# A recurrent block and its output product, put into one written order

## Chip, cores and metric

The kernel runs on one core of a Trainium2 chip. The metric is the device time of one execution in microseconds (us). The engines are TensorE (PE in the profile; PEld is its weight load), VectorE (DVE), ScalarE (ACT), GpSimd (POOL) and SyncE (SP), which here issues all DMAs.

## The reference, cut to what matters

A trunk of two layers on 1024 tokens of 1024 features, float32. Layer 0 is a gated linear recurrence, layer 1 a banded attention; a squared-ReLU MLP of 4096 hidden features follows each. The change lies in layer 0's recurrent block and in the first steps of both MLPs:

```python
def recurrent_block(x, w_in, conv_w, conv_b, w_gate, b_gate, lam, w_out):
    u = x @ w_in                                    # x is rmsnorm(h, a_norm)
    gate, rec = u[..., :D_RNN], u[..., D_RNN:]
    rec = causal_depthwise_conv(rec, conv_w, conv_b)   # four taps over tokens
    h = rg_lru(rec, w_gate, b_gate, lam)
    return (jax.nn.gelu(gate) * h) @ w_out

def rg_lru(x, w_gate, b_gate, lam):                 # eight blocks of 128 features
    g = einsum('bsnd,nde->bsne', x, w_gate) + b_gate
    r, i = sigmoid(g[..., :LRU_BW]), sigmoid(g[..., LRU_BW:])
    log_a = -LRU_C * r * softplus(-lam)
    a = exp(log_a)
    b = sqrt(-expm1(2.0 * log_a)) * (i * x)
    return associative_scan over tokens of h = a * h + b

h = h + recurrent_block(rmsnorm(h, a_norm[l]), ...)
h = h + square(relu(rmsnorm(h, mlp_norm[l]) @ w_up)) @ w_down
```

## The kernel before

Features lie on partitions (128 at a time, `NF` = 8 tiles of them), tokens along the free dimension, in two halves of 512 (`H2`). Every float32 product is made of three float32r matmuls: each operand is split into a high half (a ScalarE copy to float32r) and a low half (a VectorE or GpSimd subtraction); `mm` (lines 319 to 324) multiplies high by high, low by high, high by low into one PSUM bank. A 128x128 weight block against 512 tokens is thus three matmuls, and a whole output tile from 1024 features and 1024 tokens 48.

Order. Most of the kernel is ordered by the framework's scheduler, which simulates the engines with its own costs and takes instructions by the order in which the program traced them. Two stretches are written as chains for a planner of the kernel's own (`Plan`, line 65): each chain is a generator that issues instructions and yields the time from which it goes on; `Flag` and `Sema` are its events and counts; the instructions go into the engines' queues in the planned order. Before, these are the start (lines 526 to 543) and the attention.

The recurrent block before:

- Start: each token tile is loaded, split into halves with the norm's gain but without the norm, and multiplied at once with the first two `w_in` blocks (`first_blocks`). Beside it GpSimd squares the tokens, VectorE adds them up (line 490), an all-ones matmul sums over partitions (line 494), and ScalarE and VectorE make R, minus the reciprocal root (lines 497 to 506).
- `rec_proj` (line 547) makes one block of `rec`: 48 matmuls, then per half VectorE takes the product out of PSUM times -R (line 557) into a tile with three columns of history (lines 554, 556).
- `conv` (line 569): one ScalarE activation and three VectorE steps per half (line 578), then the split.
- `gates` (line 585) and `lru` (line 603): gate products, sigmoid, tanh, exponential, square root on ScalarE, the rest on VectorE, two multiplies on GpSimd (lines 598, 616), and the scan (line 618). All per half.
- `gelu_gate` (line 624): 48 matmuls, per half times -R (line 630), gelu, times the recurrence's result (line 632), split.
- Weights: `prepared` (line 264) splits them; for most `w_in` blocks the low half is GpSimd's (line 288).
- `Out.whole` (line 716): `w_out` product; `first` adds the residual, `last` squares and sums for the next norm, and `combine` (line 690) makes the operands of the MLP from a pair of tiles.

The MLP uses a seven-product (Strassen-like) scheme: `mlp_up` (line 737) needs seven combinations XT[0..6] of its input, each for four pairs of tiles, and per quarter four weight tiles A11 to A22 and sums of them made by GpSimd (lines 766 to 769). It asks for both norms R first (line 740), and so for their two all-ones matmuls (lines 353, 354).

## Time and profile before

| | us |
|---|---|
| median of 3 runs (2179.67 to 2182.55) | 2181.44 |
| profiled execution | 2182.72 |
| its span, first to last instruction | 2180.9 |

| engine | busy us | share of the span |
|---|---|---|
| TensorE matmul | 2112.1 | 97% |
| TensorE weight load | 1742.7 | 80% |
| VectorE | 1579.6 | 72% |
| ScalarE | 1114.8 | 51% |
| GpSimd | 661.4 | 30% |

Matmuls are pipelined, so a row of the timeline is longer than the step to the next one, and busy TensorE is not TensorE at its peak: the step between starts is what counts. The rows the text rests on stand below, in groups.

### The profile page before, as it was taken

What the parts mean: (1) busy time and instruction counts of PE and PEld (TensorE: products, weight loads), DVE (VectorE), ACT (ScalarE), POOL (GpSimd) and SP (SyncE); (2) the same over time, 40 slices, a digit from 0 to 9 for tenths busy, and PEclk for the clock granted to TensorE, in tenths of its full rate; (3) what the DMA queues carried; (4) which work ended last, traced back from release to release, by engine and by line L of the source; (5) the groups of instructions that cost most, each with busy time, mean ns of one, the idle gap of its engine ahead of it and who ended that gap; (6) DMA issues with size and microseconds to landing.
All of it is one profiled execution on the core that took longest, in us unless ns stands there. A gap on an engine that the chain in (4) does not pass through costs nothing.

```text
span 2180.9 us, 29620 instructions
## 1 busy us (share of the span) xinstructions
PE 2112.1 (97%) x9753; PEld 1742.7 (80%) x9753; DVE 1579.6 (72%) x2716; ACT 1114.8 (51%) x2030; POOL 661.4 (30%) x567
## 2 busy tenths in 40 slices
PE   7898998999999999998999999999899999999999
PEld 5776786888888888886888888878688888888887
DVE  7788866877777786555777777777687777777843
ACT  4576745444444445454666666665444344444632
POOL 5354301333320000115666666651233333000000
PEclk8999999999999999999999999999999999999999
DMA  5111144444459785442333333353354444977832
GB/s 180 32 53 37 34 141 130 156 155 155 154 179 325 244 264 179 127 150 69 96 94 82 89 84 83 89 167 109 119 178 152 150 155 155 331 263 234 258 105 97
DMA packets 176746, 319.21 MB, mean 146 GB/s; under 512 B 20816, under 2 KB 23120, under 8 KB 176592
## 3 DMA queue, kind: packets, MB, share of 16 engines
q1 hardware_dynamic: 176592, 317.33, 45.3%
q8 instruction: 76, 1.25, 0.2%
q14 instruction: 78, 0.64, 0.1%
HBM read 219.73 MB, written 78.64 MB: 137 GB/s over the span
## 4 chain that ended last, share of the span: by engine, by line
PE 78%; DVE 10%; DMA 4%; ACT 3%; issue 3%; POOL 2%; SPq 0%; DVEq 0%; ACTq 0%; POOLq 0%
PE pj L322 12%; PE pj L324 11%; PE pj L323 11%; PE tp L323 6%; PE tp L322 6%; PE tp L324 6%; PE sc L322 5%; PE sc L323 5%; PE sc L324 4%; PE tp L1178 2%; DVE c L578 2%; PE po L1206 1%; DMA s<-in_xT 1%; PE po L1205 1%; PE sc L1153 1%
## 5 line engine op out<-in xcount | busy, mean ns | idle before, releaser
L322 PE MATMUL pj<-h,wh 128*128 128x512 f32 x1269 | 510.3, 402 | 4.4 <-ACT h L338 1.6
L323 PE MATMUL pj<-l,wh 128*128 128x512 f32 x1269 | 497.1, 392 | 1.6 <-DVE l L339 1.6
L324 PE MATMUL pj<-h,wl 128*128 128x512 f32 x1269 | 496.8, 392 | 0.0
L733 ACT ACTIVATE wh<-raw 128x512 fp32r<-128x512 f32 x352 | 221.5, 630 | 335.8 <-PE tp L323 77.7
L734 DVE TENSOR_TENSOR wl<-raw,wh 128x512 fp32r<-128x512 f32 x352 | 276.5, 786 | 106.2 <-ACT wh L733 101.7
L322 PEld LDWEIGHTS pj<-h,wh 128*128 128x128 f32 x1269 | 240.0, 189 | 51.0 <-DVE s L782 2.4
L324 PEld LDWEIGHTS pj<-h,wl 128*128 128x128 f32 x1269 | 239.4, 189 | 51.5
L323 PEld LDWEIGHTS pj<-l,wh 128*128 128x128 f32 x1269 | 240.4, 189 | 43.7 <-DVE l L339 2.5
L323 PE MATMUL tp<-l,wh 128*128 128x512 f32 x657 | 257.7, 392 | 2.2 <-DVE l L336 2.1
L322 PE MATMUL tp<-h,wh 128*128 128x512 f32 x657 | 258.2, 393 | 0.4 <-ACT wh L733 0.4
L324 PE MATMUL tp<-h,wl 128*128 128x512 f32 x657 | 257.6, 392 | 0.0
L322 PE MATMUL sc<-h,wh 128*128 128x512 f32 x569 | 224.1, 394 | 6.8 <-DVE rec L557 6.8
L323 PE MATMUL sc<-l,wh 128*128 128x512 f32 x569 | 223.9, 393 | 3.0 <-DVE l L336 3.0
L324 PE MATMUL sc<-h,wl 128*128 128x512 f32 x569 | 223.4, 393 | 0.0
L336 DVE TENSOR_TENSOR l<-raw,h 128x512 fp32r<-128x512 f32 x224 | 153.6, 693 | 30.0 <-ACT h L335 28.8
L766 POOL TENSOR_TENSOR raw<-raw,raw 128x512 f32<-128x512 f32 x32 | 52.2, 1632 | 397.7 <-DVE wl L734 376.8
L748 ACT ACTIVATE s<-s 128x512 f32<-128x512 f32 x128 | 80.2, 629 | 170.9 <-DVE s L747 170.9
L335 ACT ACTIVATE h<-raw 128x512 fp32r<-128x512 f32 x224 | 137.2, 620 | 56.8 <-DMA raw<-hid 33.1
L323 PEld LDWEIGHTS tp<-l,wh 128*128 128x128 f32 x657 | 124.6, 190 | 29.7 <-DVE l L336 3.3
L322 PEld LDWEIGHTS tp<-h,wh 128*128 128x128 f32 x657 | 124.4, 189 | 27.3 <-ACT wh L733 1.0
L324 PEld LDWEIGHTS tp<-h,wl 128*128 128x128 f32 x657 | 124.4, 189 | 26.6 <-DVE wl L734 0.6
L288 POOL TENSOR_TENSOR wl<-raw,wh 128x512 fp32r<-128x512 f32 x74 | 106.1, 1439 | 118.0 <-ACT wh L285 111.6
(262 smaller groups left out, 3971.5 us busy)
## 6 DMA issues: line engine op xcount, KB each, us to landing
hid<-s SPq DMA_DIRECT2D x224, 256.0 KB, 2.0
raw<-hid SPq DMA_DIRECT2D x224, 256.0 KB, 3.6
raw<-in_w_down SPq DMA_DIRECT2D x192, 256.0 KB, 3.5
raw<-in_w_up SPq DMA_DIRECT2D x128, 256.0 KB, 2.6
s<-in_w_down SPq DMA_DIRECT2D x64, 256.0 KB, 4.5
raw<-in_w_kv SPq DMA_DIRECT2D x32, 256.0 KB, 3.3
raw<-in_w_in SPq DMA_DIRECT2D x31, 256.0 KB, 3.1
od<-ev SPq DMA_DIRECT2D x48, 128.0 KB, 2.3
```

What stands on the lines that cost most here:

```text
L288: eng.tensor_tensor(wl, raw, wh.bitcast(F32), ALU.subtract)
L322: pe.matmul(ps, lhsT=wh, rhs=xh, start=start, stop=False, skip_group_check=more)
L323: pe.matmul(ps, lhsT=wh, rhs=xl, start=False, stop=False, skip_group_check=more)
L324: pe.matmul(ps, lhsT=wl, rhs=xh, start=False, stop=stop, skip_group_check=more)
L335: act.activation(h, src, AF.Copy)
L336: dve.tensor_tensor(l, src, h.bitcast(F32), ALU.subtract)
L578: dve.scalar_tensor_tensor(ct, rec[h][:, k : k + H2], vec[:, V_CW + k, n : n + 1], ct, ALU.mult, ALU.add)
L733: act.activation(wh, raw, AF.Copy)
L734: dve.tensor_tensor(wl, raw, wh.bitcast(F32), ALU.subtract)
L748: act.activation(out, out, AF.Square)
L766: pool.tensor_tensor(raw[A11], raw[A11], raw[A21], ALU.add)
L1178: pe.transpose(pt[:, g * P : (g + 1) * P], sc[:, (kb - kb0) * P : (kb - kb0 + 1) * P], ident)
```

## The change

- The start, all eight blocks, the `w_out` product and the pair work for the MLP become one planned stretch. It ends before the last pair's combinations.
- Tokens are normalised before they are split (`halve`), so products come out of PSUM finished: no `rec` tile, no times -R. Squares move to ScalarE. The first three `w_in` blocks (two `rec`, one gate) are multiplied together, half by half. Warm-up matmuls go from 9 to 24.
- PSUM is four tiles of 1024 columns; `conv`, `lru`, `gate` and the output's add work on 1024 columns at a time, the convolution straight from PSUM. They share `NB` = 7 buffers (`bf`) and `NX` = 4 (`xf`) of 1024 columns. `+ 1` goes to ScalarE. Low halves of `w_in` weights go from GpSimd to VectorE.
- 84 of the `w_out` matmuls (two tiles, seven of eight features) come before the last Y, and the last two tiles are multiplied side by side.
- Two weight tiles of the first MLP quarter are fetched and split in the stretch; the other sums are traced before the last pair's combinations. Pools opened later reuse the first ones' memory, with waits by tile.
- For both MLPs: one ScalarE copy less in a pair's combinations, the weight sums in another order, and R asked for after four products.

```diff
-SQA = ((6, 1), (7, 1))
-WARM = 9
+NB = 7
+NX = 4
+NRAW_A = 3
+NW_A = 10
+WARM = 24
...
+    def square(k, h):
+        yield arrived[k, h]
+        if (k, h) == (0, 1):
+            yield normal[0,]
+        elif h:
+            yield squared[k - 1, h]
...
+    def halve(k, h):
+        yield normal[h,]
...
+        dve.tensor_tensor(x, x, R[h], ALU.mult)
+        yield plan.use("dve", d_(H2))
...
+        act.activation(hi, x, AF.Copy, scale=g)
...
+        dve.scalar_tensor_tensor(lo, x, g, hi.bitcast(F32), ALU.mult, ALU.subtract)
...
+    def conv(n, ps):
+        yield plan.now + LAT
+        if n >= 2:
+            yield posted[n - 2,]
+        yield bs
+        c = bf("c")
+        act.activation(
+            c, ps, AF.Identity,
+            scale=vec[:, V_CW + 3, n : n + 1], bias=vec[:, V_CB, n : n + 1],
+        )
+        yield plan.use("act", a_(T))
+        for k in range(3):
+            d = 3 - k
+            dve.scalar_tensor_tensor(
+                c[:, d:], ps[:, : T - d], vec[:, V_CW + k, n : n + 1], c[:, d:], ALU.mult, ALU.add
+            )
+            yield plan.use("dve", d_(T)) - LAT
+        pss.release(plan.t + LAT)
+        yield plan.t + LAT
+        yield bs
+        yield bs
+        ch, cl = bf("ch", F32R), bf("cl", F32R)
...
+    def lru(n, psr, psi):
+        yield plan.now + LAT
+        for _ in range(3):
+            yield bs
+        posted[n,].set(plan.t)
+        r, i, t = bf("sig"), bf("sig"), bf("tanh")
+        c = C[n][0]
+        act.activation(r, psr, AF.Sigmoid, bias=vec[:, V_BR, n : n + 1])
...
+        act.activation(i, psi, AF.Sigmoid, bias=vec[:, V_BI, n : n + 1])
...
+        act.activation(t, r, AF.Tanh, scale=sp4[:, n : n + 1])
...
+        pool.tensor_tensor(i, i, c, ALU.mult)
+        bs.release(plan.use("pool", p_(T)))
...
+        act.activation(r, r, AF.Exp, scale=sp8[:, n : n + 1])
+        act.activation(r, r, AF.Identity, bias=ones[:, 0:1])
...
+        dve.scalar_tensor_tensor(u, t, 1.0, r, ALU.add, ALU.mult)
+        dve.scalar_tensor_tensor(u, u, 4.0, r, ALU.subtract, ALU.mult)
...
+        act.activation(t, t, AF.Sqrt, scale=0.25)
...
+        dve.tensor_scalar(r, u, -0.5, -1.0, ALU.mult, ALU.add)
...
+        dve.scalar_tensor_tensor(t, t, -1.0, u, ALU.mult, ALU.mult)
...
+        pool.tensor_tensor(t, t, i, ALU.mult)
...
+        dve.tensor_tensor_scan(u, r, t, 0.0, ALU.mult, ALU.add)
...
+    def gate(n, ps):
...
+        act.activation(g, ps, AF.Gelu_apprx_tanh)
...
+        yield hidden[n,]
+        dve.tensor_tensor(g, g, HID[n], ALU.mult)
...
+    def tensor():
...
+        for n in range(1, NF + 1):
+            if 2 <= n + 1 < NF:
+                yield pss
+                ps = bank2()
+                yield from block(ps, widx[NF + n + 1], X, allk, True, True)
+                plan.start(conv(n + 1, ps))
+            m = n - 1
+            yield conved[m,]
+            yield pss
+            yield pss
...
+            plan.start(lru(m, *pair))
+            if m:
+                yield pss
+                ps = bank2()
+                yield from block(ps, widx[m], X, allk, True, True)
+                plan.start(gate(m, ps))
...
+        for j in range(2):
+            yield pss
+            ahead[j] = bank2()
+            yield from block(ahead[j], widx["out", j], Y, range(NF - 1), True, False)
...
+    def ahead_weights():
+        yield out_y[NF - 2,]
+        for x in (A11, A12):
...
+            dma(raw, w_up[0, 0, x])
...
-            b12, b21, b22 = sf(), sf(), sf()
+            b12, b22, t1, t3 = self.scratch()
+            self.XT[0][i] = split(x11, ga)
+            self.XT[1][i] = split(x21, gb)
...
-            self.XT[0][i] = split(x11, ga)
-            self.XT[1][i] = split(b21)
...
+            dve.scalar_tensor_tensor(t1, x21, gb, t1, ALU.mult, ALU.add)
+            self.XT[3][i] = split(t1, -1.0)
...
+    def up_sums(raw):
+        pool.tensor_tensor(raw[A11], raw[A11], raw[A21], ALU.add)
+        pool.tensor_tensor(raw[A21], raw[A21], raw[A22], ALU.add)
+        s1 = wsplit(raw[A21])
...
-        R = [o.r(0), o.r(1)]
+        R = []
...
+            if not R:
+                R.extend((o.r(0), o.r(1)))
...
+    first_stage.close()
+    rp = ctx.enter_context(tc.tile_pool(name="rp", bufs=NRAW, reuse_waits="tile"))
...
+    ws0 = up_weights(0, 0, FIRST_W)
+    sums0 = up_sums(ws0[0])
+    o1.combine(NF // 2 - 1)
```

In `FirstOut`, `result` adds a tile of the output to the residual, writes it to memory, squares and sums it; `combined` makes a pair's operands as `combine` does, as a chain of the plan.

## Rows read from the trace of the kernel before

**Rows 1.** The page: the span, and TensorE's busy tenths in 40 slices of the span.

```profile
span 2180.9 us, 29620 instructions
...
PE   7898998999999999998999999999899999999999
```

**Rows 2.** Busy time by stage, TensorE: stretch, length, busy (matmuls), clock, DMA share, GB/s.

```profile
0.00:57.95 57.95, 45.79 (x157) 0.88 0.52 176
57.95:281.33 223.38, 199.93 (x818) 0.95 0.14 46
281.33:350.39 69.06, 67.48 (x298) 1.00 0.42 127
350.39:390.00 39.61, 34.80 (x128) 0.87 0.40 136
372.40:1000.00 627.60, 626.86 (x2763) 1.00 0.56 185
1559.00:1584.00 25.00, 18.88 (x55) 0.80 0.36 119
```

**Rows 3.** The same view, blocks: PE, PEld, DVE, ACT, POOL busy, then the clock.

```profile
75.00:262.00 187.00, 170.58 (x707) 135.65 (x705) 159.61 (x213) 134.96 (x191) 85.62 (x53) 0.96 0.13 40
```

**Rows 4.** TensorE's waits, 0 to 400 us: us in total, times, longest.

```profile
PE po L494 <- DVE acc L490: 7.8, 1, 7.8
PE sc L322 <- DVE rec L557: 6.8, 3, 3.1
```

**Rows 5.** Groups by line, VectorE, 75 to 262: busy us, mean ns, idle before.

```profile
L578 DVE SCALAR_TENSOR_TENSOR c<-rec,vec,c 128x512 f32<-128x512 f32 x42 | 39.7, 944 | 0.9 <-ACT c L573 0.3
...
L632 DVE TENSOR_TENSOR s<-s,q 128x512 f32<-128x512 f32 x14 | 12.5, 913 | 0.0
...
L557 DVE SCALAR_TENSOR_TENSOR rec<-sc,rneg 128x512 f32<-128x512 f32 x5 | 3.4, 675 | 0.7 <-PE sc L324 0.7
```

**Rows 6.** Groups by line, ScalarE and GpSimd, 75 to 262.

```profile
L285 ACT ACTIVATE wh<-raw 128x512 fp32r<-128x512 f32 x23 | 13.9, 620 | 8.6 <-PE sc L323 5.5 <-PE tp L323 3.0
...
L592 ACT ACT_TABLE_LOAD x7 | 9.0, 1283 | 0.1
...
L616 POOL TENSOR_TENSOR tanh<-tanh,sig 128x512 f32<-128x512 f32 x15 | 26.4, 1776 | 65.7 <-DVE tanh L615 65.7
L566 POOL TENSOR_TENSOR gw<-graw,gw 128x256 fp32r<-128x256 f32 x5 | 6.6, 1327 | 6.1 <-ACT gw L563 6.1
```

**Rows 7.** Timeline, single instructions: start us, us, engine, line, operation.

```profile
5.66 1.04 POOL L481 TENSOR_TENSOR s<-x 128x512 f32<-128x512 f32 x1 [1.07 <-DMA x<-in_xT]
6.24 0.40 ACT L452 ACTIVATE w<-raw 128x256 fp32r<-128x256 f32 x1
7.17 0.41 DVE L454 TENSOR_TENSOR w<-raw,w 128x256 fp32r<-128x256 f32 x1
...
25.01 1.53 DVE L490 TENSOR_TENSOR acc<-acc,s 128x512 f32<-128x512 f32 x1
28.57 0.68 DVE L490 TENSOR_TENSOR acc<-acc,s 128x512 f32<-128x512 f32 x1
...
47.54 1.02 PE L494 MATMUL po<-acc,onesr 128*128 128x512 f32 x2
51.37 0.69 DVE L506 SCALAR_TENSOR_TENSOR rneg<-s,rneg 128x512 f32<-128x512 f32 x1
52.10 0.16 DVE L404 TENSOR_SCALAR e<-vec 128x8 f32<-128x8 f32 x1
...
266.76 1.26 DVE L618 TENSOR_TENSOR_SCAN q<-sig,q,tanh 128x512 f32<-128x512 f32 x1
```

**Rows 8.** Busy time by stage, all engines, the first 10 us.

```profile
0.00:10.00 10.00, 6.87 (x15) 4.27 (x15) 3.08 (x5) 4.30 (x7) 3.50 (x14) 1.00 0.67 208
```

**Rows 9.** Timeline, TensorE at the start of layer 1's MLP.

```profile
1565.12 0.50 PE L353 MATMUL po<-ah,onesr 128*128 128x512 f32 x1 [1.28 <-ACT ah L347]
...
1577.24 0.77 PE L353 MATMUL sc<-ah,onesr 128*128 128x512 f32 x1 [2.72 <-ACT ah L347]
```

More of the change, by code (lines that the diff above doesn't have):

```diff
@@ L1 @@
 import heapq
+import itertools
 from contextlib import ExitStack
@@ new lines, in tile_yoco_rglru_chunk_attention, with load_half, split_half @@
+    wsrc = [w_in[x] for x in worder] + [w_out[j] for j in range(NF)]
+    widx = {x: i for i, x in enumerate(worder)}
+    widx.update({("out", j): 2 * NF + j for j in range(NF)})
+    IN_G = (2, 3)
+    def load_half(i, y):
+        raw = blocks4(rawf())
+        dma(raw, wsrc[i][:, 4 * y : 4 * y + 4, :])
+        plan.start(split_half(i, y, raw), plan.load(4 * P))
+    def split_half(i, y, raw):
+        if i not in IN_G:
+            yield wss
+            yield wss
+        get = gr if i in IN_G else wr
+        wh, wl = blocks4(get("wh")), blocks4(get("wl"))
+        W[i, y] = wh, wl
+        act.activation(wh, raw, AF.Copy)
+        yield plan.use("act", a_(H2))
+        dve.tensor_tensor(wl, raw, wh.bitcast(F32), ALU.subtract)
+        last = plan.use("dve", d_(H2))
+        raws.release(last)
+        weighed[i, y].set(last)
@@ new lines, in block @@
+    def block(ps, i, Z, ks, start, stop):
+        for y in range(2):
+            mine = [k for k in ks if k // 4 == y]
+            if not mine:
+                continue
+            yield weighed[i, y]
+            for h in range(2):
+                for k in mine:
+                    if Z is Y:
+                        yield out_y[k,]
+                    w = W[i, y]
+                    mm(
+                        ps[:, hs(h)], (w[0][:, k % 4, :], w[1][:, k % 4, :]), Z[k][h],
+                        start and k == ks[0], stop and k == ks[-1],
+                    )
+                    yield plan.pe(3 * H2) - LAT
+            if i not in IN_G and mine[-1] % 4 == 3:
+                wss.release(plan.now)
+                wss.release(plan.now)
@@ L526, in tile_yoco_rglru_chunk_attention @@
-    with tc.manual_schedule(engines=set(ENG)):
-        idle = bank("sc")
-        wide = onesr.unsqueeze(1).broadcast_to([P, 4, P])
-        for x in range(WARM):
-            pe.matmul(idle, lhsT=onesr, rhs=wide, start=x == 0, stop=x == WARM - 1)
-        plan.start(loads())
-        for h in range(2):
-            for k in range(NF):
-                plan.start(halve(k, h))
-                plan.start(square(k, h))
-        for h in range(2):
-            plan.start(rstd(h))
-        plan.start(first_blocks())
-        plan.run()
@@ L639, in tile_yoco_rglru_chunk_attention @@
[L639 to L652 removed]
+                for x in range(3):
+                    yield weighed[x, k // 4]
+                    yield halved[k, h]
+                    w = W[x, k // 4]
+                    mm(recs[x][:, hs(h)], (w[0][:, k % 4, :], w[1][:, k % 4, :]), X[k][h], k == 0, k == NF - 1)
+                    yield plan.pe(3 * H2) - LAT
@@ new lines, in tensor @@
+        for _ in range(NG - 4 * NF - 4):
+            goods.release(plan.now)
+        plan.start(ahead_weights())
+        ahead = {}
+        for j in range(2):
+            yield pss
+            ahead[j] = bank2()
+            yield from block(ahead[j], widx["out", j], Y, range(NF - 1), True, False)
+        for j in range(NF - 2):
+            if j in ahead:
+                ps = ahead[j]
+                yield from block(ps, widx["out", j], Y, range(NF - 1, NF), False, True)
+            else:
+                yield pss
+                ps = bank2()
+                yield from block(ps, widx["out", j], Y, allk, True, True)
+            plan.start(o1.result(j, ps))
@@ L654, in out_order @@
+    FIRST_W = []
+    A11, A12, A21, A22 = range(4)
     def out_order(j0):
@@ L656, in out_order @@
         return full + [(j, h) for h in range(2) for j in range(NF - 2, NF)]
-    A11, A12, A21, A22 = range(4)
     class Out:
@@ L752, in mlp_up @@
             if q < NQ:
-                raw = [wload(w_up[layer, q, x]) for x in range(4)]
-                a11, a12, a22 = wsplit(raw[A11]), wsplit(raw[A12]), wsplit(raw[A22])
+                raw, (a11, a12), a22 = up_weights(layer, q) if ws is None else ws
+                ws = None
                 z, v = bank("pj"), bank("sc")
```

631 lines of the change are left out of this document (383 added, 248 removed).

## The prediction

> **What bounds the kernel now.** First the page's head and its slices: TensorE is busy 97% of the span and its row falls below 9 mostly in the first seven slices of 54.5 us, so what can be won lies where it is not dense [rows 1]. Then busy time by stage, the view that carries this prediction [rows 2]. Its second last row is the first MLP and what follows, with nothing in the way: 2763 matmuls in 627.6 us, 0.2271 us each at 512 columns. At that step the 1248 matmuls of the recurrent block and output product (768 for `w_in`, 96 for the gates, 384 for `w_out`) are 283.4 us. They end at 350 us. What each stretch takes beyond its matmuls:
>
> - 0 to 57.95 (144 matmuls beside nine of warm-up and four of the norm): 57.95 - 32.7 = 25.2 us
> - 57.95 to 281.33, the eight feature blocks (816): 223.4 - 185.3 = 38.1 us
> - 281.33 to 350.39, the output product (298): 1.4 us
> - 350.39 to 390, the hand-over to the MLP (128): 10.5 us
> - 1559 to 1584, the same hand-over in layer 1 (55): 12.5 us
>
> The third view says why the blocks are not dense: from 75 to 262 VectorE is busy 159.6 of 187 us, 85%, and TensorE's clock is down to 0.96 [rows 3]. The list of waits agrees: TensorE's longest there is for `rec` (line 557), VectorE's copy of a product out of PSUM, which every projection needs before its bank is free [rows 4].
>
> **The blocks, part by part.** A block is 108 matmuls, 24.5 us. I count what each engine has to do in it. A 1024-column instruction is not in the trace; I take the 512-column one plus the step from 256 to 512: ScalarE 0.40 to 0.62, so 1.06 us; VectorE 0.41 to 0.68, so 1.22 us; the scan 1.26, so 2.4 us; GpSimd 1.04 alone, so 2.1, or twice its mean of 1.78 beside VectorE, 3.55 us [rows 6, 7].
>
> VectorE: removed are the two `rec` products with the norm, the copy, the two products of the gelu input with the norm, and the `+ 1` (to ScalarE). Left are three convolution steps, the low half of c, two steps of u, one of t and the gate product, 8 x 1.22 = 9.8; the `r` step 0.7; the scan 2.4; and 512-column low halves, four of weights (up to now mostly GpSimd's) and two of Y, 6 x 0.68 = 4.1. Sum 17.0 us. To that comes what GpSimd costs it. The convolution step with two SBUF operands averages 0.944 us where PSUM-fed line 557 takes 0.675, and line 632 0.913 [rows 5]: some 35% on such instructions with GpSimd busy 85.6 of 187 us. GpSimd falls to two multiplies and one gate weight, 5.5 to 8.4 us of 24.5, and only 10.9 us of VectorE's list has two SBUF operands, since the convolution now reads PSUM. So +2.3: 19.3 of 24.5 us, 79%.
>
> ScalarE: nine 1024-column instructions 9.5, six halves 3.7, the gate weight 0.4, four table loads at 1.28 [rows 6] 5.1: 18.7 us, 76%. The table loads stay as many as before. No engine but TensorE fills the block.
>
> **The loop that is added.** One block's `lru` takes three of the seven 1024-column buffers; four are held by c of this block and c, ch, cl of the next. So the next `lru` starts after this one's scan, whatever TensorE does. Its length: table load and three activations 4.5; table load, exponential and `+ 1` 3.4 (the square root runs beside the next); two steps of u 2.4; r and t 1.9; GpSimd's multiply 2.1 to 3.55; scan 2.4: 16.7 to 18.2 us. Behind each of five changes of engine it can find another chain's instruction in the queue, one of about 1 us: 22 to 23. That is under 24.5, so the loop keeps up. The first turn has no gate product and is 13.6 us long, so it starts about 8.5 us late and wins 2 us a turn back; a PSUM bank is missed only from 8.6 us on (a gate product of 10.9 less 2.3 to the first sigmoid's end). At the end the last Y must come while TensorE does the last gate product and the 84 `w_out` matmuls put ahead of it: 10.9 + 19.1 = 30.0, against the loop 22, the gate product and its halves 3.2 and what is left of the lag, 0 to 5. I take 9 us lost in the blocks in place of 38.1: 4 at that end, 3 for lag, 2 for the first turn. Ends: nothing lost, and 53 us if the loop takes 31 (7 turns x 6.5 + 8 at the end).
>
> A rule of the Trainium skill speaks against the wide multiplies. What the trace shows: the same add of line 490 takes 1.53 us while GpSimd multiplies and 0.68 when it does not [rows 7]. The page "SBUF — State Buffer", section "Who interferes with whom", says that a VectorE instruction with two SBUF inputs and a GpSimd instruction that reads SBUF hold one shared port pair in turn, each for its whole length. By that, twice as long a multiply is twice as long a block for whoever comes second, and u, t and the scan could each wait 3.5 us; the time would be that of the slower rival below. The same section says that one SBUF input does not contend, and line 557 agrees.
>
> **The start.** Before, the first product starts on raw tokens as they come; now it waits for the norm. 208 GB/s came in over the first 10 us [rows 8], 2.1 MB, which is the eight half rows of the tokens. Square 0.62, add 0.68, then from the sum's matmul to the norm 4.5 us (47.54 to 52.06) [rows 7]: 16 us; product 0.68 and high half 0.7: first matmul at about 17.5. 24 warm-up matmuls cover until 9. Half the 144 matmuls, 16.4, and 2 for the lower clock after an idle stretch: 36. On SyncE's queue the second half rows stand behind the fourth weight load, which waits for one of three raw buffers, that is for the first split at about 12; at 1.26 us each they land by 22. The second half's norm comes when VectorE has done eight token products and low halves 10.9, seven adds 4.8, five weight halves 3.4, the norm 1.4 and half of some thirty constants at 0.16 [rows 7] 2.5, 23.0 after 16.5: with its first half 40.9. Then 16.4: 57.3. So this costs what it did; I take 57, 24 lost. Ends: 50 with no second wait, 66 if weights take half the early bandwidth (10 us) and each add meets a queue.
>
> **The output and the hand-over.** The product itself has 1.4 us to lose; its results are added at 1.22 us each 10.9 us apart, and a pair's combinations are eleven VectorE instructions of 0.69, 7.6 us in 21.8, so 1.4 stays; ends 0 and 6. At its end the two last results (2.4), a split (1.4) and the queues come to about 6 us; ready then are A11 and A12 and three of four pieces of two products, 18 matmuls, 4.1. 2 lost, 1 for the next pieces, 1.5 for the sums of the other two weights (their loads stand behind two result writes), 1.5 for the clock (0.87 in this stretch before [rows 2]): 6 in place of 10.5; ends 3 and 15. The DMAs moved are the same loads. They cost nothing while those 18 matmuls last.
>
> **Layer 1.** Norm sums are now asked for behind the first four products. TensorE waited 1.28 and 2.72 for their high parts [rows 9]; 4 us go, next late is the low half of the last tokens. 9 in place of 12.5; ends 5 and 14. One scalar copy less in a pair costs or wins nothing there.
>
> **Sum.** 25.2 to 24, 38.1 to 9, 10.5 to 6, 12.5 to 9: 38.3 us less. The profiled execution took 2182.72 (span 2180.9), 1.3 above the median of 2181.44. 2182.7 - 38.3 - 1.3 = 2143. The attention and MLP stretches have the same code and the same 0.2271.
>
> **Rivals.**
> 1. The added loop rules, slower. From 30 us on, 7 x 5.5 + 8 = 47 lost eats all (29.1 + 9.2 + 9). If u, r and t, and the scan each wait 3.5 us for GpSimd, 18.2 + 10.5 + 5 is 33.7; at 33 the blocks lose 67.5 where I have 9: 2143 + 58 = 2201. Against it: GpSimd's own two multiplies fall where the loop's VectorE part stands still, so only the gate weight, 1.33 us [rows 6], can meet it. For it: ScalarE's queue is in order, and the convolution two blocks on waits in it for the buffer that GpSimd's first multiply frees; the exponential of the same loop stands behind it, so a late multiply stops the loop itself.
> 2. The loop is a little long, 27 us: 7 x 2.5 + 8 = 25.5 lost, 2160. Or the start takes 66 and the hand-over 15: 2161.
> 3. Nothing is won: VectorE just stays the limit at 24.5 + 4.8 us a block, as now (38.1 / 8): 2172, with start or hand-over bad 2181.
> 4. Nearly dense: blocks lose 1, start ends at 52, hand-over 3: 2143 - 8 - 5 - 3 = 2127.
> 5. It does not do what it says: the weights for the MLP's other products are not fetched until the writes are out. Hand-over 15: 2152, inside the range.
>
> **Chances.** The forecast, 2132 to 2152: 0.52. Rival 2 and 5, to 2172: 0.22. Rival 4: 0.13. Rival 3: 0.05. Rival 1: 0.08. Nothing under 0.2% (4.4 us) can be told from no change. Below 2177: 0.88; within: 0.04; above 2186: 0.08. The range leaves out rival 1 and 3, and the far side of 4: 2121 to 2172.
>
> **What would show it.** Right: TensorE over 95% busy from the 144th matmul to the 1248th, its end near 318 us, VectorE near 79% in the blocks and no wait on a `rec` copy. The loop step is wrong if the first sigmoid regularly starts after the scan before it and TensorE waits for a bank then. The start step is wrong if the first projection matmul is far from 17.5 or the second half's from 41. The hand-over step is wrong if TensorE waits over 3 us for a sum of weights. The whole is wrong if the MLP's steady stretches no longer step at 0.2271.

## The result

The changed kernel takes 2160.26 us (median of 4 runs, 2157.57 to 2161.16) where the kernel before took 2181.27 beside it: 0.9905 of it, 95% interval 0.9893 to 0.9917. That is 21 us faster. The forecast was 38 us faster, 2143; the range of 2121 to 2172 holds the time, which lies above the narrower 2132 to 2152 and in the band of rivals 2 and 5.

The page of the profile after, its execution 2157.57 us, answers to [rows 1]: the span, the busy time of each engine, and in 40 slices of 54 us TensorE's busy tenths and its granted clock.

```profile
span 2155.8 us, 29333 instructions
PE 2099.2 (97%) x9768; PEld 1738.2 (81%) x9768; DVE 1543.8 (72%) x2600; ACT 1113.8 (52%) x1971; POOL 583.2 (27%) x511
...
PE   7999998999999999998999999989899999999999
...
PEclk8999999999999999999999999999999999999999
```

The dips in slices two and four are gone; the first slice and the one of the hand-over to the MLP (the seventh) are left. Busy time by stage, TensorE, columns as in [rows 2]:

```profile
0.00:60.77 60.77, 49.37 (x171) 0.86 0.38 128
60.77:258.10 197.33, 188.43 (x816) 0.98 0.15 48
258.10:323.40 65.30, 65.30 (x290) 1.00 0.40 133
323.40:365.00 41.60, 32.20 (x117) 0.88 0.55 184
```

The eight blocks take 197 us in place of 223, the output product is dense. The start takes 3 us more than before, and the hand-over, 117 products of 0.2271 us in 41.6, leaves 15.0 us unused: more than before.

The same view with all engines, most of the blocks and then one block of 24.5 us, answers to [rows 3] (busy of PE, PEld, DVE, ACT, POOL; clock; DMA share; GB/s):

```profile
70.00:255.00 185.00, 176.10 (x761) 144.31 (x761) 134.34 (x116) 138.31 (x148) 47.12 (x22) 0.98 0.15 47
129.10:153.60 24.50, 24.50 (x110) 20.27 (x109) 18.20 (x17) 18.14 (x20) 5.57 (x3) 1.00 0.16 49
```

In a steady block TensorE has no gap. VectorE is busy 18.2 of 24.5 us, 74% (85% before), ScalarE 18.1, GpSimd 5.6. The groups of VectorE and GpSimd, 60 to 325 and 60 to 260 us, answer to [rows 5, 6]: the convolution step, the scan and the two multiplies.

```profile
L607 DVE SCALAR_TENSOR_TENSOR c<-p,vec,c 128x1021 f32<-128x1021 f32 (+2 forms) x24 | 30.5, 1275 | 0.9 <-ACT c L600 0.7
L659 DVE TENSOR_TENSOR_SCAN q<-sig,tanh 128x1024 f32<-128x1024 f32 x8 | 21.0, 2620 | 2.3 <-POOL tanh L655 2.3
...
L655 POOL TENSOR_TENSOR tanh<-tanh,sig 128x1024 f32<-128x1024 f32 x8 | 20.1, 2514 | 42.0 <-DVE tanh L653 32.5 <-DMA raw<-in_w_out 9.5
L637 POOL TENSOR_TENSOR sig<-sig,c 128x1024 f32<-128x1024 f32 x8 | 19.4, 2430 | 61.5 <-ACT sig L631 52.4 <-DMA graw<-in_w_gate 9.2
```

1.28 us for a convolution step (1.22 was my estimate, and what most other wide steps take), 2.62 for the scan (2.28 where nothing disturbs it, 2.4 estimated), 2.43 and 2.51 for the multiplies, between my 2.1 and 3.55. TensorE's waits from 0 to 400 us answer to [rows 4]; no wait on `rec` is left, and the one for the norm's sum is 2.8 us for 7.8:

```profile
PE p L332 <- ACT h L587: 5.9, 2, 5.6
PE tp L332 <- ACT wh L1001: 4.0, 1, 4.0
PE p L332 <- DVE c L607: 3.2, 1, 3.2
PE tp L363 <- ACT ah L357: 2.9, 1, 2.9
PE p L557 <- DVE acc L549: 2.8, 1, 2.8
```

The first is the start (the first projection waits for a token's high half). The second is the hand-over (the high part of a sum of weights), the fourth the norm behind it, and the third the first turn of the blocks.

For every kernel below I counted what TensorE lost in a stage: the time from the start of one 512-column product to that of another in the trace, less 0.2271 us for each between them (products of the warm-up and the norms are left out of the count). Stages: the first 144 products; the next 816; after the 288 of the output (-0.1 in every kernel), 128 of the hand-over; and 380 around layer 1's hand-over. By this count the kernel before lost 13.2 and not 10.5 at the hand-over, and 14.3 in layer 1: the cut lies elsewhere than in [rows 2]. The stages are those of one traced execution each. The traced one of the kernel before took 2182.72 us and that after 2157.57, 25 us apart where the medians are 21 apart, so the stages make the gain look up to 4 us larger.

| kernel | median us | of before [95%] | start | blocks | hand-over | layer 1 |
|---|---|---|---|---|---|---|
| before | 2181.27 | 1 | 25.3 | 38.0 | 13.2 | 14.3 |
| after | 2160.26 | 0.9905 [0.9893, 0.9917] | 28.5 | 12.5 | 16.2 | 10.4 |
| r0, after again | 2160.02 | 0.9909 [0.9896, 0.9923] | 29.5 | 14.0 | 16.8 | 11.2 |
| e1 MLP edits alone | 2173.18 | 0.9962 [0.9948, 0.9976] | 24.8 | 36.4 | 6.6 | 9.8 |
| e2 norms first | 2167.07 | 0.9937 [0.9925, 0.9950] | 29.1 | 12.7 | 19.9 | 15.1 |
| e3 weights early | 2163.93 | 0.9922 [0.9910, 0.9935] | 29.8 | 13.7 | 19.8 | 11.0 |
| e4 512 columns | 2167.39 | 0.9940 [0.9927, 0.9953] | 29.5 | 18.7 | 16.2 | 10.9 |
| e5 low halves on GpSimd | 2160.82 | 0.9913 [0.9895, 0.9931] | 30.8 | 14.1 | 16.2 | 10.9 |
| e7 fill | 2164.05 | 0.9921 [0.9908, 0.9933] | 32.2 | 12.9 | 16.1 | 12.3 |
| e8 VectorE relief | 2167.59 | 0.9932 [0.9919, 0.9946] | 33.3 | 14.2 | 16.9 | 11.1 |
| e9 long loop | 2200.88 | 1.0091 [1.0074, 1.0108] | 29.1 | 53.4 | 16.2 | 11.8 |
| e11 TensorE sums | 2158.43 | 0.9901 [0.9888, 0.9915] | 26.7 | 12.9 | 16.1 | 11.3 |
| e12 sums on VectorE | 2158.19 | 0.9898 [0.9885, 0.9912] | 28.8 | 14.0 | 14.2 | 10.9 |
| e13 writes later | 2159.57 | 0.9904 [0.9891, 0.9918] | 28.1 | 12.9 | 16.1 | 10.7 |

The two traces of the changed kernel differ by up to 1.5 us in a stage, so a stage tells differences from about 2 us on. The kernel before, run again beside each group of experiments, took 2180.61 to 2181.75, so medians of different groups compare to about 1 us beyond their own scatter.

### The profile page after: what moved, and what is told of

The parts are those of the page before. It is cut to its first block, busy times and chain, and to the rows that moved or that the text cites. A ratio compares the mean times of both kernels' runs of the same rounds, so it can differ in the third digit from the quotient of the medians.

```text
span 2155.8 us, 29333 instructions
## 1 busy us (share of the span) xinstructions
PE 2099.2 (97%) x9768; PEld 1738.2 (81%) x9768; DVE 1543.8 (72%) x2600; ACT 1113.8 (52%) x1971; POOL 583.2 (27%) x511
## 4 chain that ended last, share of the span: by engine, by line
PE 87%; DVE 5%; ACT 3%; issue 2%; DMA 1%; POOL 1%; SPq 0%; DVEq 0%; POOLq 0%; ACTq 0%
PE pj L332 12%; PE pj L333 12%; PE pj L334 12%; PE tp L333 6%; PE tp L332 6%; PE tp L334 6%; PE sc L334 4%; PE sc L333 4%; PE sc L332 4%; PE p L333 4%; PE p L332 3%; PE p L334 3%; PE tp L1486 2%; PE po L1514 1%; PE po L1513 1%
## 5 line engine op out<-in xcount | busy, mean ns | idle before, releaser
L332 PE MATMUL pj<-h,wh 128*128 128x512 f32 x1205 | 482.8, 401 | 2.5 <-DVE s L1064 1.0
L332 PE MATMUL tp<-h,wh 128*128 128x512 f32 x569 | 223.9, 393 | 7.0 <-ACT wh L1001 4.0
L334 PE MATMUL tp<-h,wl 128*128 128x512 f32 x569 | 223.5, 393 | 1.0 <-DVE wl L1002 1.0
L333 PE MATMUL tp<-l,wh 128*128 128x512 f32 x569 | 223.8, 393 | 0.3 <-DVE l L346 0.3
L332 PE MATMUL p<-h,wh 128*128 128x512 f32 x384 | 153.3, 399 | 10.8 <-ACT h L587 5.9
L332 PE MATMUL sc<-h,wh 128*128 128x512 f32 x418 | 162.8, 389 | 0.1
L334 PE MATMUL sc<-h,wl 128*128 128x512 f32 x418 | 162.8, 389 | 0.0
L333 PE MATMUL sc<-l,wh 128*128 128x512 f32 x418 | 162.6, 389 | 0.0
L333 PE MATMUL p<-l,wh 128*128 128x512 f32 x384 | 153.2, 399 | 4.2 <-DVE l L683 2.4
L334 PE MATMUL p<-h,wl 128*128 128x512 f32 x384 | 151.9, 396 | 0.0
```

What stands on the lines that cost most here:

```text
L332: pe.matmul(ps, lhsT=wh, rhs=xh, start=start, stop=False, skip_group_check=more)
L333: pe.matmul(ps, lhsT=wh, rhs=xl, start=False, stop=False, skip_group_check=more)
L334: pe.matmul(ps, lhsT=wl, rhs=xh, start=False, stop=stop, skip_group_check=more)
```

## The experiments

### The changed kernel again

> The changed kernel itself once more, beside the next three on the same chip, so that differences of 2 to 5 us can be read. 2160 us, 0.9893 to 0.9917 of the kernel before; the first projection product, at 18.66 us in the trace after, came at 19.1 to 21.2 in kernels whose start was not touched before it, so I expect it 0.5 to 1.2 us later here.

2160.02 us. The first projection came at 19.57 us, 0.9 later than in the first trace. What follows is compared with both traces.

### The hand-over: where do its 16 us come from?

**Weights early (e3).**

```diff
 def ahead_weights():
     for x in (A11, A12):
-        raw, wh, wl = rawf(), gr("wh"), gr("wl")
+        raw, wh, wl = gf("raw"), gr("wh"), gr("wl")
         dma(raw, w_up[0, 0, x])
...
+    for x in (A21, A22):
+        yield goods
+        RAW0.append(gf("raw"))
+        dma(RAW0[x], w_up[0, 0, x])
```

> The changed kernel, but all four weight tiles of the first MLP quarter (not two) are fetched and kept inside the planned stretch; nothing is computed otherwise. My theory: the hand-over of layer 0 loses 15.0 us and not 6, because the loads of these tiles are issued at 324.8 to 326.5 us, behind two result writes, GpSimd's first sum starts only at 331.75, and TensorE waits 4.02 and 1.02 us for the parts of those sums and then runs at the lower clock to 342. With the tiles there early the sums start as soon as GpSimd is free, both waits go and part of the stretch at the lower clock with them: the hand-over loses 7 to 10 us, the whole is 5 to 8 us shorter, 2152 to 2155 us (0.9868 to 0.9880 of the kernel before). Rival: the last results, their combinations and the norm end late anyway, and the wait for a sum of weights only becomes a wait for a piece of the tokens: under 2 us, 2158 to 2160.

2163.93: 3 to 4 us slower. In the changed kernel the list of single instructions shows GpSimd's first sum and TensorE's wait for it (start, length, and in brackets the idle time before with what ended it):

```profile
331.75 1.70 POOL L1012 TENSOR_TENSOR raw<-raw,raw 128x512 f32<-128x512 f32 x1 [85.85 <-DMA raw<-in_w_up]
...
335.83 0.72 PE L332 MATMUL tp<-h,wh 128*128 128x512 f32 x1 [4.02 <-ACT wh L1001]
...
338.00 0.80 PE L334 MATMUL tp<-h,wl 128*128 128x512 f32 x1 [1.02 <-DVE wl L1002]
```

With the tiles there early the same view shows:

```profile
342.78 0.50 PE L332 MATMUL sc<-h,wh 128*128 128x512 f32 x1 [2.87 <-ACT wh L1006]
347.45 0.80 PE L334 MATMUL sc<-h,wl 128*128 128x512 f32 x1 [3.94 <-DVE wl L1007]
```

The wait for the first quarter's sums is gone, and longer ones for the second quarter's weights stand in its place (6.8 us for 5.0). So the late transfer is what TensorE is seen waiting for, and taking it away wins nothing: something behind it is as late. The rival said under 2 us won; a loss was expected by neither theory. Four more tiles were taken from the buffers that the combinations of the last pairs also use, which may be a part of it.

**Writes later (e13).**

```diff
-            dma(self.keep[j], x)
+            if j < NF - 2:
+                dma(self.keep[j], x)
...
     ws0 = up_weights(0, 0, FIRST_W)
+    for j in (NF - 2, NF - 1):
+        dma(x1d[j], o1.xs[j])
```

> The changed kernel with the writes of the two last results (512 KB each) issued behind the four loads of the first MLP quarter, not ahead of them; the result is the same. Theory D (the transfer is late, my rival 5 and the term of 1.5 us): the loads land 3 to 5 us earlier, GpSimd's first sum starts at 327 to 329 in place of 331.75, and of TensorE's 4.02 and 1.02 us of waiting and the lower clock behind them 4 to 6 us go: layer 0's hand-over takes 15.0 - 5 = 10. Theory C (VectorE's list): the sums start earlier, but the high and low parts of the weights and the last tokens still stand in VectorE's queue to 345 us: under 1.5 us.

2159.57, no difference that can be told. One write still left first, at 324.38, and the four loads went at 324.81 to 326.64 (324.80 to 327.88 in the changed kernel); GpSimd's first sum came 7.2 us after the last output product (7.5 and 8.6 in the two traces of the changed kernel), TensorE waited 3.33 and 0.37 us for 4.02 and 1.02, and then 1.29 more for the next weights. So the two writes had held the loads up by 1.2 us at most, and their order in the queue is not the cause. The expectation had put 3 to 5 us on it; loads that land much earlier were tried in e3 alone.

**Sums on VectorE (e12).**

```diff
-    sums0 = up_sums(ws0[0])
+    sums0 = up_sums(ws0[0], dve)
...
-            s1, s2 = up_sums(raw) if sums is None else sums
+            s1, s2 = up_sums(raw, pool if q else dve) if sums is None else sums
```

> The changed kernel with the four sums of weights of each layer's first MLP quarter on VectorE in place of GpSimd; the result is the same. Theory C (VectorE is the bound of the hand-over: it is busy without a gap from 324 to 345 us, and four of its instructions take 1.75 us beside GpSimd's sums, 1.07 too much each): VectorE's list changes by 4 x 0.68 - 4 x 1.07 = -1.6 us, the chain of sums is 4 us shorter, and each hand-over is 2 to 4 us shorter: 3 to 7 us won in all. Theory D (the transfer of the weights is late): the sums still cannot start before 331.75, and their four 0.68 us push the low halves of the tokens back: layer 0 wins under 1 us or loses 1 to 3.

2158.19, 1.8 us less than the changed kernel beside it, where theory C had 3 to 7; the intervals overlap. The stage count puts the gain where it was expected: the hand-over loses 14.2 for 16.2 and 16.8. In layer 1 nothing can be told (10.9 for 10.4 and 11.2). So GpSimd's sums cost some 2 us of the 16, at the edge of what a stage can tell.

**MLP edits alone (e1)**, in the kernel before:

```diff
-        R = [o.r(0), o.r(1)]
+        R = []
...
+            s1 = wsplit(raw[A21])
             pool.tensor_tensor(raw[A22], raw[A22], raw[A11], ALU.add)
+            s2 = wsplit(raw[A22])
             pool.tensor_tensor(raw[A12], raw[A12], raw[A22], ALU.add)
-            s1, s2 = wsplit(raw[A21]), wsplit(raw[A22])
...
+            if not R:
+                R.extend((o.r(0), o.r(1)))
```

(with the combinations rewritten as in the change).

> The kernel before with only the MLP's edits: the combinations rewritten, the sums of weights split as they come, the norms asked for behind the first four products. With the norms asked for first again in the changed kernel, the hand-over of layer 0 took 3.6 us more and that of layer 1 4.6 us more. Theory: that gain is the edit's own and does not need the planned stretch: 4 to 9 us less than the kernel before, 2172 to 2177 (0.996 to 0.998). Rival: it is worth something only where the last results come as early as in the changed kernel; then layer 1 alone, 3 to 4.6 us: 2177 to 2178.5, and layer 0's hand-over stays at 10.5 us lost.

2173.18, 7.6 us less than the kernel before: the theory. The table says more than I asked: without the planned stretch the hand-over loses only 6.6 us, 6.6 less than before, where I had forecast 4.5 less for the changed kernel. So the edits do what I said, and the planned stretch takes it back and 3 us more. (This trace is of the fastest of five executions, 2170.29, and 12.4 us below the traced one before, so 4 to 5 us of the differences by stage are scatter; the 9.6 to the changed kernel is more than that.) Busy time by stage, all engines, 21.5 us from the last output product, here and then in the changed kernel and with the sums on VectorE:

```profile
344.50:366.00 21.50, 18.09 (x72) 14.20 (x71) 17.36 (x24) 13.06 (x23) 7.01 (x4) 0.92 0.28 86
```

```profile
324.30:346.00 21.70, 15.24 (x51) 10.35 (x50) 20.91 (x27) 12.90 (x21) 9.00 (x6) 0.84 0.57 194
```

```profile
326.20:348.00 21.80, 16.13 (x58) 11.29 (x57) 21.37 (x31) 13.62 (x22) 3.60 (x3) 0.92 0.58 193
```

In e1 TensorE does 72 matmuls there, in the changed kernel 51, and VectorE is full: 20.9 of 21.7 us, 96%, for 17.4 (81%). Two things weigh more on it than in e1. Its instructions grow beside GpSimd, ahead of the first sums of weights; these are VectorE's in the changed kernel:

```profile
333.92 1.75 DVE L1002 TENSOR_TENSOR wl<-raw,wh 128x512 fp32r<-128x512 f32 x1
...
336.19 1.76 DVE L1002 TENSOR_TENSOR wl<-raw,wh 128x512 fp32r<-128x512 f32 x1
337.87 1.76 DVE L346 TENSOR_TENSOR l<-sc,h 128x512 fp32r<-128x512 f32 x1
```

In e1 two instructions grow as much, but 16 us behind the product; the first of the two:

```profile
360.21 1.79 DVE L706 SCALAR_TENSOR_TENSOR s<-xr,vec,s 128x512 f32<-128x512 f32 x1
```

And the last two results come whole, 1024 columns each, around the product's end (added at 323.11 and 324.85), so the last pair's combinations, splits and sums of squares all fall behind it at once; in e1 the four half results are added at 337.95, 341.76, 346.40 and 350.29 around the product's end at 344.5, the last of them later than in the changed kernel. The loads are early there as well: four of the MLP's weight tiles are issued from 301 to 341 us, in the changed kernel the first quarter's (two of them a second time) only when the stage's buffers come free, from 324.80 on. With e3, e12 and e13 each taking one cause away for a gain of 2 us at most, what is left between 14.2 and 6.6 was not taken apart: that the full results at the end, or VectorE's full list, are the cause is my reading of the traces and was not tried, and neither were two of the causes removed together.

**Norms first (e2).**

```diff
-        R = []
+        R = [o.r(0), o.r(1)]
...
-            if not R:
-                R.extend((o.r(0), o.r(1)))
```

> The changed kernel, but the MLP asks for both norms ahead of its first product again, as the kernel before did. If the deferral is what took layer 1 from 12.5 us lost to 9.6, as I forecast (TensorE's waits of 1.28 and 2.72 us at the norm's sums), they come back: 3 to 4 us longer, 2163 to 2164 (0.9918 to 0.9924), with waits over 1 us for the sum's high part near 1560 us. Rival: the next late thing (the low half of the last tokens) holds TensorE anyway, and the rewritten combinations brought the gain: under 1 us, 2160 to 2161.

2167.07, 7.0 us longer than r0, twice what I expected: 3.1 in layer 0 and 3.9 in layer 1. TensorE's waits from 1510 to 1590 us in it:

```profile
PE sc L363 <- ACT ah L357: 7.1, 1, 7.1
PE tp L332 <- ACT wh L1001: 1.2, 1, 1.2
```

and in the changed kernel:

```profile
PE tp L332 <- ACT s L1057: 3.0, 1, 3.0
PE pj L333 <- DVE l L349: 2.9, 1, 2.9
```

With the norms deferred the wait for a norm's high part [rows 9] is gone, and the low half of the last tokens is late next (2.9), as forecast. Beside it stands a wait of 3.0 that was not: ScalarE's copy of a product (L1057) comes behind the deferred norm's own steps in ScalarE's queue. Layer 0 had its share in it, which the prediction booked at nothing.

### The blocks: why are they dense, and how near is the limit?

**Long loop (e9).**

```diff
         pool.tensor_tensor(t, t, i, ALU.mult)
+        pool.tensor_tensor(t, t, i, ALU.mult)
+        pool.tensor_tensor(t, t, i, ALU.mult)
```

> The changed kernel with GpSimd's second multiply of the recurrence done three times (the recurrence then gets t times i cubed, so the output is another). It makes only the loop longer, by two multiplies of 2.4 to 2.7 us: from 22.7 to 27.5 to 28. Theory, the price of my rival 1 and 2: what passes 24.5 us is paid in seven turns and once more at the end, 7 x 3.2 + 5 = 27 us; the blocks lose 35 to 42 us in place of 12, the whole is 2183 to 2190 (1.001 to 1.004). Other theory: the lag does not reach TensorE, since four banks, the projections and the products put ahead cover it; then only the end pays, 5 to 10 us, 2165 to 2170. Third: VectorE's contention with GpSimd adds 1.07 us to each instruction that it meets, some three more a block, and VectorE stays under 22 of 24.5 us: nothing by itself.

2200.88: the blocks lose 53.4 us, where 35 to 42 were expected. ScalarE's table loads ahead of the first sigmoids, in the changed kernel and then in e9, show the turns:

```profile
139.75 1.28 ACT L629 ACT_TABLE_LOAD   x1
164.24 1.28 ACT L629 ACT_TABLE_LOAD   x1
188.72 1.28 ACT L629 ACT_TABLE_LOAD   x1
```

```profile
132.23 1.28 ACT L629 ACT_TABLE_LOAD   x1
...
190.29 1.28 ACT L629 ACT_TABLE_LOAD   x1
...
248.97 1.28 ACT L629 ACT_TABLE_LOAD   x1
```

In the changed kernel a turn is 24.5 us, TensorE's own block. In e9 (which takes the blocks in pairs, one row of each pair shown) it is 58.4 / 2 = 29.2. Two multiplies of 2.4 to 3.3 us were added, so the changed kernel's loop is near its limit. In it the scans end at 138.04, 163.75 and 188.37, and the table loads of the next turn start 1.7, 0.5 and 0.35 us later; the second of these scans:

```profile
161.47 2.28 DVE L659 TENSOR_TENSOR_SCAN q<-sig,tanh 128x1024 f32<-128x1024 f32 x1
```

My price of seven turns and 8 at the end is 7 x 4.7 + 8 = 41 us; the blocks lost 40.9 and 39.4 more than in the two traces of the changed kernel. The price holds, but on top of what they lose otherwise. It is TensorE's waits (60 to 290 us) that pay it, for the convolution and at the end for the last Y:

```profile
PE p L332 <- DVE c L607: 16.8, 3, 6.0
PE p L332 <- ACT h L683: 12.3, 1, 12.3
PE p L332 <- ACT ch L616: 6.2, 1, 6.2
```

The second theory, a lag that does not reach TensorE, falls.

**512 columns (e4).**

```diff
-        act.activation(t, r, AF.Tanh, scale=sp4[:, n : n + 1])
+        for s in HV:
+            act.activation(t[:, s], r[:, s], AF.Tanh, scale=sp4[:, n : n + 1])
...
```

and so for every wide instruction of the block.

> The changed kernel with every 1024-column instruction of the convolution, the recurrence and the gate product as two of 512 columns; the result is the same. By the durations, the width saves 0.18 us on each of nine ScalarE instructions (1.06 for 2 x 0.62), 0.14 on each of eight of VectorE (1.22 for 2 x 0.68) and 0.24 on the scan: a block's VectorE list goes from 18.2 to 19.6 us and ScalarE's from 18.1 to 19.7, both under the 24.5 us of TensorE, and the loop from first sigmoid to scan from 22.7 to 24 to 25. Theory: the width is not what the change lives by; under 3 us lost, 2160 to 2164 (0.9900 to 0.9920). Rival: the loop passes 24.5 us because of it and is paid seven times and at the end: 2168 to 2180, with TensorE waiting for a bank in the later blocks.

2167.39, 7.4 us longer than r0; 5 to 6 of them in the blocks. I expected under 3: it is the rival, just under its range. VectorE and ScalarE stay under the block (37.8 and 39.2 us busy from 145.00 to 195.10), but the turn passes 24.5. Its table loads:

```profile
118.26 1.28 ACT L635 ACT_TABLE_LOAD   x1
145.00 1.28 ACT L635 ACT_TABLE_LOAD   x1 [4.41 <-DVE q L677]
166.04 1.28 ACT L635 ACT_TABLE_LOAD   x1
195.10 1.28 ACT L635 ACT_TABLE_LOAD   x1 [1.36 <-DVE q L677]
```

Two turns wait for the scan before them (`DVE q`), and from 118.26 to 195.10 a turn is 25.6 us. The width is worth 5 to 7 us, not for the busy time that it saves but for the loop.

**Low halves on GpSimd (e5).**

```diff
-        dve.tensor_tensor(wl, raw, wh.bitcast(F32), ALU.subtract)
-        last = plan.use("dve", d_(H2))
+        eng = pool if 3 <= i < 2 * NF else dve
+        eng.tensor_tensor(wl, raw, wh.bitcast(F32), ALU.subtract)
+        last = plan.use("pool", p_(H2)) if eng is pool else plan.use("dve", d_(H2))
```

> The changed kernel with the low halves of the block's projection weights on GpSimd again, as before, about four of them in a block of 24.5 us; the result is the same. VectorE's list falls from 18.2 us by 4 x 0.68 = 2.7, GpSimd's rises from 5.6 by 4 x 1.6 to 1.8 = 6.8. Theory: the two engines lengthen each other (a VectorE instruction takes 1.75 for 0.68 us beside GpSimd at the hand-over), a multiply of the loop can stand behind a weight's low half, and the loop goes from 22.7 to 25 to 27 us: 7 to 18 us lost, 2167 to 2178 (0.993 to 0.998). Rival: the loop stays under 24.5 us and nothing is lost, 2159 to 2162; then which of the two engines takes the halves does not matter.

2160.82, the same as the changed kernel: the rival. Busy by engine from 141 to 190 us, and groups of VectorE from 60 to 260:

```profile
141.00:190.00 49.00, 49.00 (x218) 40.59 (x217) 32.84 (x23) 36.19 (x40) 25.81 (x16) 1.00 0.17 54
```

```profile
L660 DVE TENSOR_TENSOR_SCAN q<-sig,tanh 128x1024 f32<-128x1024 f32 x8 | 23.1, 2890 | 6.4 <-POOL tanh L656 6.3
...
L676 DVE TENSOR_TENSOR ge<-ge,q 128x1024 f32<-128x1024 f32 x8 | 14.5, 1818 | 0.2
```

GpSimd is busy 25.8 of 49 us (12.4 in the changed kernel from 139.75 to 188.72), and VectorE's instructions do grow (the gate product 1.82 us for 1.22, the scan 2.89 for 2.62), but TensorE has no gap. VectorE has 16 us to spare there, and the extra work fell beside the loop. GpSimd's share is thus 53%, more than the 46% of the kernel before [rows 3], so a GpSimd as busy as before does not by itself hold the blocks up. So that the change moved these halves to VectorE is not why it is faster.

### The start: the clock or VectorE's list?

**Fill (e7).**

```diff
-WARM = 24
+WARM = 32
+FILL = 22
...
+        if h == 0:
+            for x in range(FILL):
+                pe.matmul(both[:, hs(1)], lhsT=onesr, rhs=wide, start=x == 0, stop=x == FILL - 1)
```

> The changed kernel with 32 warm-up products in place of 24 and 22 more products without use behind the first norm sum, so that TensorE does not stand idle before its first projection; the result is the same. Theory A: the lower clock (0.58 and 0.56 granted from 10 to 30 us) sets the start, since TensorE's 9 products of a token take 3.9 us at the 0.43 us step of that stretch and 2.04 at 0.2271: the 144 projection products end 4 to 6 us before 60.8, the whole is 2154 to 2156 (0.9876 to 0.9885). Theory B, to which I give more weight: the low halves of the first half's tokens come 2.2 to 4.8 us apart (18.73, 23.54, 27.17, 30.53, 32.76, 35.57, 39.35, 41.49) from VectorE's queue, which also holds seven sums of squares, weight halves and some thirty constants; TensorE waits for them at either clock: 0 to 2 us, 2158 to 2160 (0.9895 to 0.9905).

2164.05, 3 to 4 us longer, and no test of the clock: the filling products write the bank that ScalarE reads the norm's sum from, so ScalarE waited for all of them, and TensorE stood idle behind them. ScalarE's row, then TensorE's:

```profile
18.57 0.69 ACT L566 ACTIVATE rneg<-p,eps 128x512 f32<-128x512 f32 x1 [5.70 <-PE p L564]
```

```profile
24.11 0.80 PE L333 MATMUL p<-h,wh 128*128 128x512 f32 x1 [5.65 <-ACT h L592]
```

The granted clock was 1.00 from 10 to 20 us and 0.66 from 20 to 30 (0.58 and 0.56 in the changed kernel). The first projection came 5.5 us late, the 144th product 3.7.

**VectorE relief (e8).**

```diff
-            dve.tensor_tensor(xsq[0, h], xsq[0, h], q, ALU.add)
+            (pool if h else dve).tensor_tensor(xsq[0, h], xsq[0, h], q, ALU.add)
```

and sixteen of the small constants likewise.

> The changed kernel with two kinds of VectorE instructions of the start on GpSimd, which is idle then: the seven sums of the second half's squares (0.60 us a step each) and sixteen of the small constants (0.16 each); the result is the same. By theory B (VectorE's list sets the start) 4.2 + 2.6 = 6.8 us leave VectorE before 38 us, the second half's norm comes 4 to 7 us earlier, and the 144 products end near 55 to 57 in place of 60.8: 2154 to 2156 (0.9876 to 0.9885). By theory A (the clock sets it) TensorE at the lower clock needs 3.9 us a token and does not go faster: under 1.5 us, 2159 to 2160. A third way: GpSimd's sums beside VectorE make VectorE's token products longer, as line 490 was before (1.53 for 0.68 us), and nothing is won or up to 3 us lost, 2160 to 2163.

2167.59, 5 us longer by the ratios and 7 by the medians: the third way, at more than its price. The low halves of tokens, 0.75 us alone, and the token products, 0.68, in e8's VectorE:

```profile
27.29 1.76 DVE L592 SCALAR_TENSOR_TENSOR l<-x,gneg,h 128x512 fp32r<-128x512 f32 x1
28.97 0.68 DVE L585 TENSOR_TENSOR x<-x,rneg 128x512 f32<-128x512 f32 x1
30.45 1.71 DVE L592 SCALAR_TENSOR_TENSOR l<-x,gneg,h 128x512 fp32r<-128x512 f32 x1 [0.79 <-ACT h L589]
```

What meets one of GpSimd's sums takes 1 us more, and GpSimd, at 1.3 to 1.6 us a sum, finishes later: the second norm came at 46.7 and not 39.4. By the table 3.8 to 4.8 us are the start's.

**TensorE sums (e11).**

```diff
+        if h:
+            act.activation(q.bitcast(F32R), xin[k, h], AF.Square)
...
+            pe.matmul(xsq[0, h], lhsT=onesr, rhs=q.bitcast(F32R), start=k == 0, stop=k == NF - 1)
...
         yield small(dve.tensor_tensor, e2, e1, e1, ALU.mult)
+        yield normal[1,]
```

> The changed kernel with VectorE's list at the start shortened without GpSimd: the second half's squares are summed by eight products on TensorE (the squares in TensorE's reduced float32 form, a slightly other rounding of the norm), and the small constants wait for the second norm. 7 x 0.60 + some 17 x 0.17 = 7 us leave VectorE before 38 us. If VectorE's list sets the start (theory B): the second norm comes at 32 to 34 in place of 38, the 72nd product at 40 to 42 in place of 44.7 (from there the clock and TensorE's own 2.04 to 3.9 us a token), the 144th near 57 in place of 61: 3 to 5 us won. If the clock sets it: the second norm comes early all the same, but the 72nd product stays at 44 to 45 and the 144th at 60 to 61: under 1 us.

2158.43, 1.6 us less than r0; the intervals overlap, but the trace agrees: the second norm is there at 34.6 us (39.4 in the changed kernel), the 72nd product starts at 42.8 (44.7 and 45.6; 44.2 to 46.0 in eight traces with the same code at the start), the 144th at 59.1 (61.0 and 61.9). Theory B said 57. TensorE from 20 to 30 us in the two traces of the changed kernel and in e11, where five of the 32 are the sums of squares:

```profile
20.00:30.00 10.00, 9.75 (x25) 0.56 0.73 258
```

```profile
20.00:30.00 10.00, 8.36 (x24) 0.78 0.72 252
```

```profile
20.00:30.00 10.00, 9.39 (x32) 0.86 0.82 286
```

In the first trace TensorE is busy there and does 25 products, at the step of the lower clock level (1.2 of 2.4 GHz: 0.43 us); it had stood idle 5.6 us just before. In the second trace the clock is back some 4 us earlier (0.78 for 0.56), and TensorE does no more: it waits for the halves of tokens instead, and its 72nd product starts 26.05 us after its first, in the first trace 26.02. So 4 us less of the lower clock win nothing, which speaks against theory A. What e11 wins goes to theory B, VectorE's list, at less than its 3 to 5 us; the clock is earlier in e11 as well, but by the two traces that alone is worth nothing. e11 and e12 have the lowest medians here; they were not put together.

## Why the prediction was right, and where its sizes were wrong

By its own terms (time beyond 0.2271 us a product):

| term | before | forecast | measured |
|---|---|---|---|
| start | 25.2 | 24 | 60.77 - 32.7 = 28.1 |
| blocks | 38.1 | 9 | 197.33 - 185.3 = 12.0 |
| output product | 1.4 | 1.4 | 0 |
| hand-over | 10.5 | 6 | 15.0 |
| layer 1 | 12.5 | 9 | 3.1 to 3.9 less than before by the count above: 9 |

The misses add up to 4.1 + 3.0 - 1.4 + 9.0 = 14.7; 2143 + 15 = 2158 is the traced execution, and the median is 2 to 3 us above it. The time is inside the range because the range reached as far as rivals 2 and 5; to their band I had given 0.22, to the narrower one 0.52.

**Blocks: right.** That no engine but TensorE is full any more, and that the new loop stands just under TensorE's block, is what the traces show: 18.2 us for VectorE (19.3 forecast), 18.1 for ScalarE (18.7), first sigmoid to scan's end 141.05 to 163.75, 22.7 (22 to 23), and no gap from 104 to 202 us. e9 shows that it is this loop that would decide, and at the price of rival 1; e4 that it is nearer the edge than the 1.5 us of slack that I gave it. In parts, the first turn lost 3.4 us (2 forecast), the lag between nothing (3), and the end 9.0 (4): there the last turns follow each other in 16 to 18 us and the last but one recurrence takes 30 (206.3 to 236.5). Which edit took the blocks from 38 to 12 was only in part taken apart: the width is worth 5 to 7 us and the engine of the low halves nothing, but tokens normalised first, wider PSUM tiles and the planned order were not tried one by one. That VectorE was what held the blocks before stays argued from its 85% and its waits. The rule of the Trainium skill ("SBUF — State Buffer", "Who interferes with whom") that speaks against the wide multiplies holds where GpSimd and VectorE meet, 1.75 us for 0.68; in the blocks e5 shows that they can meet twice as long with nothing lost.

**Hand-over: the step that failed.** I wrote "1.5 for the sums of the other two weights", and of their loads that they "cost nothing while those 18 matmuls last". The 18 products last 4.1 us; the loads leave only when the stage's buffers come free at its end, GpSimd's first sum starts 7.5 us after the last output product, and TensorE waits 4.02 and 1.02. That was my own sign for it (a wait over 3 us for a sum of weights), and rival 5 gave the size, 15. But rival 5's cause is not enough: e3 took the late loads away and e13 moved them up to 1.2 us ahead, and neither won. VectorE is full for the 21 us after the product, where I had counted two results, a split and the queues, about 6 us. I had not priced what else the planned stretch leaves for the end: e1, without that stretch, loses 6.6 us at the hand-over, where the changed kernel loses 16.2 and 16.8. Why the stretch costs that much stays open beyond the 2 us of GpSimd's sums.

**Start: 4 us missed, on another chain than the one I named.** The first projection (18.66, 17.5 forecast) and the second norm (39.4, 39.5 by the sum of the forecast) came on time. But the second half's first product started at 44.90 and not at 41, since TensorE was still at the first half: its 72 products took 26.2 us, where I had 16.4 and 2 for the lower clock. The second half then ran in 16.3, as forecast. The lower clock is not what was mis-sized: 4 us less of it change nothing between the two traces of the changed kernel. The first half's tokens come too slowly: their low halves start 2.1 to 4.8 us apart on VectorE, where nine products, a token's share, take 2.04. e11 wins 2 to 3 us by a shorter list on VectorE; what holds the rest of the chain was not taken apart.

**Layer 1: right**, by the wait that I named; e2 puts 3.9 us on it, and 3.1 more in layer 0 that I had not counted.

## What to carry to other kernels

An engine's busy share says whether it can be the limit; a chain that passes through several engines and holds its buffers to the end is a limit of its own, and its turn, read from one instruction that comes once a turn, shows how near it is. When a stage ends in a planned order, look at what its end piles up on one engine (whole results, splits, late loads), since a wait that is removed there is followed by the next one of the same engine. Moving work to an idle engine that slows the busy one can cost more than leaving it (e8), and costs nothing where neither lies in the chain that decides (e5).

## What was not expected of the hardware

A VectorE instruction of 0.68 to 0.75 us takes 1.71 to 1.76 beside a GpSimd sum of 1.3 to 1.7 us, at the hand-over and in e8 alike: 1.0 to 1.1 us more. GpSimd's own instructions on 128 x 8 elements took from 0.20 to 0.66 us in e8, where VectorE's take 0.16. And in e7 the clock, granted in full for 10 us, was back at the lower level for the first projections after an idle stretch of 5.65 us. In the changed kernel the lower level ended some 4 us earlier in one trace than in the other, and the start was no shorter for it.
